# Moving the start addresses of the resident matmul operands by 8 to 240 bytes, stage by stage

## The chip, the cores and the metric

The kernel runs on one core of one Trainium2 chip. The metric is the device time of one execution in microseconds (us). Two executions of the kernel before took 2346.87 and 2346.46 us, a median of 2346.66 us.

Engines are named as in the profile: PE is TensorE's matmul side, PEld its weight loads, DVE is VectorE, ACT is ScalarE, POOL is GpSimd, SP is SyncE (it issues most DMAs here). SBUF is the on-chip memory of 128 partitions, PSUM the matmul's accumulators. In a matmul the *stationary* operand is loaded into the array first; the *moving* operand is then streamed from SBUF through it, a column at a time. "128x512" is a matmul whose moving operand has 128 partitions and 512 columns.

## The reference

One layer over 4096 prompt rows and 32 sample rows of width 1024, all float32. The large products are the input projection (`h @ w_in`, 1024 to 5120 columns; the pooling matrix is folded into one of its parts) and the output projection (`concat(a, b) @ w_out`, 2048 to 1024):

```python
def mixer_layer(x, pool_past, pos0, norm_g, w_in, ln_v_g, ln_v_b, w_spatial, b_spatial,
                w_pool, pool_scale, w_out):
    h = rmsnorm(x, norm_g)
    proj = jnp.einsum('btd,de->bte', h, w_in)
    u, v, z_a, xb, z_b = jnp.split(proj, [W_A, 2 * W_A, 3 * W_A, 3 * W_A + W_B], axis=-1)
    v_n = layernorm(v, ln_v_g, ln_v_b)
    a = u * chunk_mlp(v_n, w_spatial, b_spatial) * jax.nn.silu(z_a)
    x_ext = jnp.concatenate([pool_past.astype(xb.dtype), xb], axis=1)
    b = pool_mix(x_ext, pos0, w_pool, pool_scale) * jax.nn.silu(z_b)
    y = x + jnp.einsum('bte,ed->btd', jnp.concatenate([a, b], axis=-1), w_out)
    return y, x_ext[:, -POOL_STATE:], v_n
```

`chunk_mlp` multiplies 128 rows of v by a masked 128x128 matrix for each of 8 heads; `pool_mix` takes trailing means of 2, 4, 8 or 16 rows. The five outputs are the two final RMSNorms of y, two small state buffers and the sample's normalised v.

## The kernel before, in words

Every large product is done in a two-by-two block scheme with seven block products in place of eight (numbered q = 0 to 6, `NQ` = 7): operands are sums and differences of quarters, and `Combine` or `OutPair.multiply` adds the seven results up. Each operand is split into a high and a low part in the float32r format, and a block product is 12 matmuls: four pieces of 128 in the contracted dimension, and for each high x high, high x low and low x high.

One operand of every block product stays in SBUF for a whole stage: seven *slots*, one for each q (pool `slots`, helper `slot()` at L105). A slot is 16,896 bytes a partition, which is 33 x 512; the built program puts the first one at byte 18,432 of a partition, which is 36 x 512, so all seven begin at a multiple of 512 bytes. The slots are always the moving operand; what changes from step to step is the stationary one (`op` in the first stage, `wop` afterwards). The stages, in order of time:

- **v stage** (about 52 to 397 us): the slots hold the v columns of `w_in` (`wv`, L264). ACT and DVE write them (`weight_ops`), PE reads a row of 512 adjacent columns, 2048 bytes. In front of it lies the folding of the pooling matrix.
- **Blocks 0, 1, 2** (three stages of about 320 us from 397, 721 and 1040 us on): 1024 prompt rows each. A slot holds the row operands, loaded from `xops` by `Tokens.load` (L922, two DMAs of 1 MB a slot) or, for block 0, by `load_first` (L589, DMAs for two of the four row groups and a DVE and an ACT copy for the others). They are laid out as `(h j k t)`, and so a matmul's moving operand is four runs of 128 columns, each 512 bytes long and 2048 bytes from the next:

```python
return self.ops[q][:, :8 * HALF].rearrange("p (h j k t) -> p h k j t", h=2, j=4, t=P)[:, h, k]
```

- **Block 3, the last** (about 1359 to 1704 us): 1024 prompt rows and the 32 sample rows. A slot is filled to its end, as `(h k t)` with t = 528 columns (`WIDE`), and a row is taken in two matmuls of 264 columns, 1056 bytes each.
- **Output projection, z = 0 and z = 1** (about 1704 to 2026 and 2026 to 2338 us): the slots hold seven combinations of one half of `w_out`, loaded from `wops` by `load_out_weights` (L632, one DMA of 2 MB a slot). PE reads 512 adjacent columns; the very last step uses 256 at a time.

In each of blocks 0 to 2 the slots are read by 16 sets of weight columns, each set 7 x 12 = 84 matmuls, 1344 in all; the v stage (16 row pairs) and each half of the output projection (16 pairs) have the same count, block 3 twice as many of the narrow ones.

The order is written out in the program. Where two sets share the end or the beginning of a stage, `lagged` interleaves their steps as a0 a1 b0 a2 b1 a3 b2 a4 a5 b3 a6 b4 b5 b6. After step q of the last set of a stage the slot of q is free, and SP issues its load for the next stage at that point (L931, L634, L596); the new stage's first set reaches q = 6 ten steps after the old stage's last step. SP's queue also carries the weight loads (L956), which stand behind these. `prepare` has DVE and ACT make the stationary operands some steps ahead of PE.

Of the kernel before, what the change touches and what calls it, by code (L numbers as in the profile page):

```python
# [9 lines left out]
F32R = mybir.dt.float32r  # L10
# [5 lines left out]
P = 128  # L16
D = 1024
# [8 lines left out]
NB = 4  # L26
TB = SEQ // NB
HALF = TB // 2
EXT = DEC // 2
WIDE = HALF + EXT  # L30
TOT = SEQ + DEC
NQ = 7
WARM = 14


@with_exitstack
def stream_step(ctx: ExitStack, tc, x_prompt, x_sample, state_pool, norm_g, w_in, ln_v_g, ln_v_b,
# [18 lines left out]
    slots = ctx.enter_context(tc.tile_pool(name="slots", bufs=NQ))  # L56
# [45 lines left out]
        return y, guess + 3 * [lambda: stt(t, y, y, m, ALU.mult, ALU.mult),  # L102
                               lambda: stt(y, t, 1.5, y, ALU.add, ALU.mult)]

    def slot():  # L105
        return slots.tile([P, 2 * 4 * WIDE], F32R, tag="slot", name="slot")


    behind = []
# [101 lines left out]
    with ExitStack() as ph:  # L211
# [23 lines left out]
        def tr_tile():  # L235
            return ps_tr.tile([P, 512], F32, tag="tr", name="tr")

        g_bc = g_p.tile([P, D], F32, name="g_bc")
        first_ops = {}
# [9 lines left out]
        warm = tr_tile()  # L249
        for _ in range(WARM):  # L250
            tc.keep_in_program_order(nc.tensor.transpose(warm[:, :P], ident, ident))
# [9 lines left out]
                mm(dst, rows[ct], wraw[g // 2][:, 2 * (g % 2) + ct, :], start=ct == 0, stop=ct == 1)  # L261


        wv = [slot()[:, :8 * HALF].rearrange("p (h k n) -> p h k n", h=2, n=HALF) for _ in range(NQ)]  # L264

        v_raws = {}

# [86 lines left out]
        class Past:  # L354


            def load(self):
                self.st = half(), half()
                for z in range(2):
                    nc.gpsimd.memset(self.st[z][:HALO], 0.0)  # L360
                    nc.sync.dma_start(self.st[z][1:HALO], state_pool[0, 0, :, z * 512:(z + 1) * 512])
# [226 lines left out]

        def load_first(q):  # L589

            first_ops[q] = t = slot()
            dst = t[:, :8 * HALF].rearrange("p (h j x) -> p h j x", h=2, j=4)
            src = xops[0].rearrange("j p (q h x) -> q h p j x", q=NQ, h=2)
            n = 2 if q < NQ - 1 else 4
            for h in range(2):
                nc.sync.dma_start(dst[:, h, :n].bitcast(F32), src[q, h, :, :n])  # L596
            if n == 4:
                return
            nc.vector.tensor_copy(dst[:, :, pa.j], pa.ops[q])
            nc.scalar.copy(dst[:, :, pb.j], pb.ops[q])  # L600
# [4 lines left out]
        for n, (pair, q) in enumerate(lagged(pa, pb)):  # L605
            for step in {0: steps[:2], 1: steps[2:3], 2: steps[3:4], 4: steps[4:5], 6: steps[5:6], 7: steps[6:]}.get(n, []):
                step()
            if n == 1:
                norms([], [(v, P) for v in pairs[-3].v])
                pairs[-3].store()  # L610
            pair.product(q)
            if pair is pb:
                load_first(q)
# [16 lines left out]
    w_slots = {}  # L630

    def load_out_weights(z, q):  # L632
        w_slots[z, q] = t = slot()[:, :4 * D].rearrange("p (k h n) -> p k h n", k=4, h=2)
        nc.sync.dma_start(t.bitcast(F32), wops[z, q].rearrange("p k (h n) -> p k h n", h=2))  # L634

    class OutWeights:
# [227 lines left out]
    with ExitStack() as ph:  # L864
# [50 lines left out]
        class Tokens:  # L915
# [4 lines left out]
                self.groups = [(0, HALF)] if not self.last else [(0, WIDE // 2), (WIDE // 2, WIDE // 2)]  # L920

            def load(self, q):  # L922
                t = slot()
                self.ops[q] = t
                if self.last:
                    nc.sync.dma_start(t.bitcast(F32), xops_l[q].rearrange("p x t -> p (x t)"))
                    return
                src = xops[self.b].rearrange("j p (q h x) -> q h p j x", q=NQ, h=2)
                for h in range(2):
                    dst = t[:, h * 4 * HALF:(h + 1) * 4 * HALF].rearrange("p (j x) -> p j x", j=4)  # L930
                    nc.sync.dma_start(dst.bitcast(F32), src[q, h])  # L931
# [214 lines left out]
        for n in range(n_sets):  # L1146
# [9 lines left out]
            for s, q in order:  # L1156
                at += 1
                prepare(at + LEAD)
                while later:
                    (later.pop(0) or (lambda: None))()  # L1160
                for c, c0, w in cs[id(s)]:
                    s.product(c, q, c0, w)
                if n == 0 and q == 0:
                    behind.append(s)
                if s is g[-1] and groups[n + 1][0].stage != s.stage:
                    if n + 1 < n_sets:
                        groups[n + 1][0].tok.load(q)
                    else:
                        if q == 3:
                            groups[n_sets][1].begin([raw_tile(), raw_tile()], True)  # L1170
                        load_out_weights(0, q)
                if n == 0 and s is g[-1] and q in (3, 5):
                    next(constants, None)
                if s.kind == "gate" and q in (2, 4):
                    if q == 2:
                        s.t1 = []
                    s.t1.append(s.spatial(len(s.t1)))
                if s.kind == "gate" and q == 6 and s.tok.last:
                    s.spatial_sample()
                if q == NQ - 1:  # L1180
                    later.append(s.finish_gate() if s.kind == "gate" else s.finish_pool())
# [4 lines left out]
    with ExitStack() as ph:  # L1186
# [56 lines left out]
        for n in range(n_sets, len(groups)):  # L1243
# [6 lines left out]
            for m, (s, q) in enumerate(order):  # L1250
                at += 1
                prepare(at + LEAD)
                if m == 0 and n in samples:
                    samples[n].load()
                k = n - n_sets - 4
                if k == KT and m == 2:
                    sample_rows()
                if 0 <= k < KT and m in (0, 2):
                    state_load(k) if m == 0 else state_split()
                s.multiply(q)  # L1260
                if n == n_sets and s is g[0] and q == NQ - 1:
                    s.finish()
                if m == 2 and ended:
                    for x in ended:
                        x.finish()
                if s is g[-1] and n + 1 < len(groups) and groups[n + 1][0].stage != s.stage:
                    load_out_weights(1, q)
                if 0 <= k < KT and m == 6:
                    state_rows(k)
# [34 lines left out]
```

## Time and profile before

The profiled execution spans 2345.9 us, from its first to its last instruction; the other two executions took 2346.87 and 2346.46 us.

| | busy us | share of the span |
|---|---|---|
| PE, matmuls | 2328.8 | 99% |
| PEld, weight loads | 1981.3 | 84% |
| DVE | 1790.2 | 76% |
| ACT | 896.4 | 38% |
| POOL | 215.1 | 9% |
| DMA, 445.69 MB | | 190 GB/s on average |

A matmul's own duration in the profile runs from its start to the end of its drain and overlaps that of the next one, so the mean of one (389 ns for 512 columns) says how long one takes and not how fast they follow one another. How fast they follow is read from a stretch without gaps: the time from the first start to the last start, divided by their number less one. That quotient is called the *pitch* below. Times of windows are counted from the span's start.

### The profile page before, as it was taken

To read this page: it belongs to the slowest core of one execution; us is meant where nothing else is said; L and a number is where in the kernel's file an instruction comes from. 1 tells how busy PE (TensorE), PEld (TensorE's weight loads), DVE (VectorE), ACT (ScalarE), POOL (GpSimd) and SP (SyncE) were. 2 spreads that over 40 slices of the span, in tenths; PEclk is the share of its full clock that TensorE was granted. 3 is DMA by queue.
4 is the path that set the end of the run, shared out by engine and by line. 5 is a ranking of instruction groups with operands and counts; after the bars stand their busy time and mean duration, and the time that the engine had idled before them with its cause. 6 is when DMAs were issued, how large, how long until landed. Compare 5 with 4: busy or idle time off the path is not lost.

```text
span 2345.9 us, 32604 instructions
## 1 busy us (share of the span) xinstructions
PE 2328.8 (99%) x11936; PEld 1981.3 (84%) x11936; DVE 1790.2 (76%) x3318; ACT 896.4 (38%) x1603; POOL 215.1 (9%) x398
## 2 busy tenths in 40 slices
PE   8999999999999999999999999999999999999998
PEld 7878888888888888888888899999987878888877
DVE  7877786866787767877668876668777778688887
ACT  6545544433433333433334333334322333233333
POOL 1010000100021000111000110102200000000000
PEclk9999999999999999999999999999999999999999
DMA  8879977432448334483334472335587776955542
GB/s 309 316 241 279 275 255 245 142 104 89 149 144 296 99 100 134 135 300 122 108 108 148 177 262 87 101 100 164 223 294 265 252 257 232 360 171 169 159 137 90
DMA packets 325145, 445.69 MB, mean 190 GB/s; under 512 B 19324, under 2 KB 248444, under 8 KB 322296
## 3 DMA queue, kind: packets, MB, share of 16 engines
q1 hardware_dynamic: 273384, 355.05, 45.9%
q0 software_dynamic: 22288, 73.48, 8.3%
q10 hardware_dynamic: 29312, 15.08, 2.4%
q8 instruction: 94, 1.54, 0.3%
q14 instruction: 67, 0.55, 0.1%
HBM read 273.88 MB, written 169.66 MB: 189 GB/s over the span
## 4 chain that ended last, share of the span: by engine, by line
PE 95%; DMA 2%; DVE 2%; issue 0%; ACT 0%; SPq 0%; ACTq 0%; DVEq 0%
PE acc L193 66%; PE acc L712 8%; PE acc L713 8%; PE acc L714 8%; PE sp L998 2%; PE tr L473 1%; DMA wops<-raw 1%; DMA vt<-in_w_in_dram 1%; PE acc L261 0%; DMA op<-in_w_in_dram 0%; PE more L844 0%; PE more L843 0%; DVE wop L81 0%; DVE y L724 0%; PE acc L202 0%
## 5 line engine op out<-in xcount | busy, mean ns | idle before, releaser
L193 PE MATMUL acc<-slot,wop 128*128 128x512 f32 (+1 forms) x6720 | 1260.9, 348 | 1.0 <-DVE wop L81 1.0
L193 PEld LDWEIGHTS acc<-slot,wop 128*128 128x128 f32 x6720 | 1081.1, 188 | 156.5 <-DVE wop L81 1.4
L81 DVE TENSOR_TENSOR wop<-raw,wop 128x512 fp32r<-128x512 f32 (+1 forms) x510 | 353.4, 695 | 133.0 <-ACT wop L119 121.7
L119 ACT CAST wop<-raw 128x512 fp32r<-128x512 f32 x340 | 210.5, 622 | 384.4 <-PE acc L193 266.9
L712 PE MATMUL acc<-slot,wop 128*128 128x512 f32 x892 | 347.2, 389 | 1.5 <-DVE y L724 1.5
L713 PE MATMUL acc<-slot,wop 128*128 128x512 f32 x892 | 347.1, 389 | 0.0
L714 PE MATMUL acc<-slot,wop 128*128 128x512 f32 x892 | 347.0, 389 | 0.0
L193 PE MATMUL acc<-slot,op 128*128 128x512 f32 x1344 | 323.8, 395 | 0.3 <-ACT vt L167 0.2
L193 PEld LDWEIGHTS acc<-slot,op 128*128 128x128 f32 x1344 | 247.6, 188 | 51.9 <-ACT vt L167 0.7
L165 DVE TENSOR_TENSOR t<-acc,t 128x512 f32<-128x512 f32 (+1 forms) x320 | 186.7, 584 | 120.0 <-ACT t L174 65.5
L724 DVE TENSOR_TENSOR y<-acc,y 128x512 f32<-128x512 f32 x235 | 159.3, 687 | 72.6 <-PE acc L714 72.2
L712 PEld LDWEIGHTS acc<-slot,wop 128*128 128x128 f32 x892 | 167.4, 188 | 37.8 <-ACT wop L677 2.3
L714 PEld LDWEIGHTS acc<-slot,wop 128*128 128x128 f32 x892 | 167.4, 188 | 34.8
L713 PEld LDWEIGHTS acc<-slot,wop 128*128 128x128 f32 x892 | 167.4, 188 | 34.7
L677 ACT CAST wop<-raw 128x512 fp32r<-128x512 f32 x160 | 98.7, 622 | 175.2 <-PE acc L714 164.9
L81 DVE TENSOR_TENSOR wop<-sum,wop 128x512 fp32r<-128x512 f32 x200 | 136.9, 685 | 25.7 <-ACT wop L119 24.9
L1017 POOL DMA_DIRECT2D abT<-t x128 | 69.2, 541 | 843.2 <-DVE t L1029 622.7
L119 ACT CAST wop<-sum 128x512 fp32r<-128x512 f32 x136 | 84.5, 622 | 96.9 <-PE acc L193 72.0
L1040 DVE TENSOR_TENSOR t<-t 128x527 f32<-128x527 f32 (+3 forms) x160 | 111.1, 698 | 0.6
L677 ACT CAST wop<-sum 128x512 fp32r<-128x512 f32 x64 | 39.7, 622 | 119.5 <-PE acc L714 96.3
L174 ACT COPY t<-acc 128x512 f32<-128x512 f32 (+1 forms) x80 | 40.2, 504 | 107.1 <-PE acc L193 105.4
L115 DVE TENSOR_TENSOR sum<-raw 128x512 f32<-128x512 f32 x68 | 46.8, 688 | 44.7 <-DMA raw<-in_w_in_dram 44.1
(236 smaller groups left out, 1955.0 us busy)
## 6 DMA issues: line engine op xcount, KB each, us to landing
raw<-in_w_in_dram SPq DMA_DIRECT2D x102, 512.0 KB, 4.3
xops<-op SPq DMA_DIRECT2D x72, 512.0 KB, 6.1
abT<-t POOLq DMA_DIRECT2D x128, 256.0 KB, 3.8
raw<-abT SPq DMA_DIRECT2D x64, 512.0 KB, 5.0
slot<-xops SPq DMA_DIRECT2D x30, 1024.0 KB, 9.6
slot<-wops SPq DMA_DIRECT2D x14, 2048.0 KB, 9.7
xt<-in_x_prompt_dram SPq DMA_DIRECT2D x32, 512.0 KB, 5.0
raw<-v_all SPq DMA_DIRECT2D x32, 512.0 KB, 3.3
```

The costliest lines, as they stand in the source:

```text
L81: return nc.vector.tensor_tensor(out, src, hi.bitcast(F32), ALU.subtract)
L119: pair = nc.scalar.copy(hi, src), lo_part(lo, src, hi)
L165: add = lambda o, x, y: nc.vector.tensor_tensor(o, x, y, ALU.add)
L193: mm(acc, stationary(s, k), moving(m, k), start=fresh and n == 0, stop=n == len(terms) - 1, skip_group_check=True)
L677: nc.scalar.copy(t[:, 0], src)
L712: mm(acc, x[:, 0, k, :], w[:, k, 0, c], start=fresh and k == 0, stop=False, skip_group_check=True)
L713: mm(acc, x[:, 0, k, :], w[:, k, 1, c], start=False, stop=False, skip_group_check=True)
L714: mm(acc, x[:, 1, k, :], w[:, k, 0, c], start=False, stop=k == 3, skip_group_check=True)
L724: nc.vector.tensor_tensor(y, self.acc[bank], y, ALU.add)
L998: mm(sp[:, a, :], self.v[:, 4 * hf + a, :], WT[:, h, :], start=True, stop=True)
L1017: nc.gpsimd.dma_start(abT[row, :, t0:t0 + HALF], t[:, :HALF])
L1040: tt(nxt[:, lo:HALO + m], s[:, lo:HALO + m], s[:, lo - step:HALO + m - step], ALU.add)
```

## The change

`slot` takes a number of float32 columns that the tile's view begins late by, and each stage gives its own:

```diff
+SHIFT = (48, 56, 60, 0, 24, 40, 2)
...
-    def slot():
-        return slots.tile([P, 2 * 4 * WIDE], F32R, tag="slot", name="slot")
+    def slot(shift=0):
+        t = slots.tile([P, 2 * 4 * WIDE], F32R, tag="slot", name="slot")
+        return t[:, shift:] if shift else t
...
-        wv = [slot()[:, :8 * HALF].rearrange("p (h k n) -> p h k n", h=2, n=HALF) for _ in range(NQ)]
+        wv = [slot(SHIFT[6])[:, :8 * HALF].rearrange("p (h k n) -> p h k n", h=2, n=HALF) for _ in range(NQ)]
...
-            first_ops[q] = t = slot()
+            first_ops[q] = t = slot(SHIFT[0])
...
-        w_slots[z, q] = t = slot()[:, :4 * D].rearrange("p (k h n) -> p k h n", k=4, h=2)
+        w_slots[z, q] = t = slot(SHIFT[NB + z])[:, :4 * D].rearrange("p (k h n) -> p k h n", k=4, h=2)
...
-                t = slot()
+                t = slot(SHIFT[self.b])
```

| stage | shift in columns | start in bytes past a multiple of 512 | a matmul reads |
|---|---|---|---|
| v stage | 2 | 8 | 1 run of 2048 bytes |
| block 0 | 48 | 192 | 4 runs of 512 bytes |
| block 1 | 56 | 224 | 4 runs of 512 bytes |
| block 2 | 60 | 240 | 4 runs of 512 bytes |
| block 3 | 0 | 0 (its slots have no room) | 1 run of 1056 bytes |
| output, z = 0 | 24 | 96 | 1 run of 2048 bytes |
| output, z = 1 | 40 | 160 | 1 run of 2048 bytes |

Rows and runs in a slot are a multiple of 512 bytes apart in all of them but block 3, so every moving operand of a stage begins by the same distance past a multiple of 512. The tiles keep their addresses and sizes, the stationary operands and PSUM tiles too. No instruction is added, removed or moved on any engine or queue: the two built programs have the same instructions in the same order, and differ in the addresses at which DMAs, ACT and DVE write the slots and PE reads them.

## Prediction

> **What bounds the kernel now.** I read the page's table of engines first, then the waits of PE, then the chain of work that ended last, and last the stretches of each stage.
>
> ```profile
> PE 2328.8 (99%) x11936; PEld 1981.3 (84%) x11936; DVE 1790.2 (76%) x3318; ACT 896.4 (38%) x1603; POOL 215.1 (9%) x398
> PE acc L712 <- DVE y L724: 1.5, 2, 1.1
> PE 95%; DMA 2%; DVE 2%; issue 0%; ACT 0%; SPq 0%; ACTq 0%; DVEq 0%
> ```
>
> PE is busy for 2328.8 of 2345.9 us. The second row is one of the longest of PE's waits on another engine after the start-up: 1.5 us in two times. The chain (third row) is PE for 95% of the span. So nothing hides a change in the matmuls' own speed, and nothing else is worth much. What the change can touch is that speed, through where the moving operand begins, and the writing of the slots.
>
> The stages as windows (stretch in us, its length, PE busy and matmuls, granted clock, DMA share, GB/s), from the v stage to the end of the output projection:
>
> ```profile
> 51.80:396.90 345.10, 344.04 (x1631) 1.00 0.84 268
> 397.00:720.50 323.50, 322.55 (x1488) 1.00 0.45 147
> 720.60:1039.70 319.10, 319.10 (x1473) 1.00 0.46 154
> 1039.80:1358.90 319.10, 319.10 (x1473) 1.00 0.46 154
> 1359.00:1704.00 345.00, 345.00 (x2831) 1.00 0.44 152
> 1704.20:2025.70 321.50, 319.98 (x1410) 1.00 0.79 272
> 2025.70:2338.20 312.50, 312.44 (x1390) 1.00 0.48 161
> ```
>
> PE has no gap worth the name in any, and the clock is full in all of them. Blocks 0, 1 and 2 are within 4.4 us of one another. The pitch inside them comes from PE's timeline (start, time from first start to last end, line, operands, count):
>
> ```profile
> 701.83 16.48 PE L193 MATMUL acc<-slot,wop 128*128 128x512 f32 x72
> 1369.84 30.38 PE L193 MATMUL acc<-slot,wop 128*128 128x264 f32 x249
> 1749.81 0.39 PE L712 MATMUL acc<-slot,wop 128*128 128x512 f32 x1
> ...
> 1755.02 0.39 PE L714 MATMUL acc<-slot,wop 128*128 128x512 f32 x1
> 2335.11 0.28 PE L712 MATMUL more<-slot,wop 128*128 128x256 f32 x1
> ...
> 2337.86 0.28 PE L714 MATMUL more<-slot,wop 128*128 128x256 f32 x1
> ```
>
> - Block 0, four runs of 512 bytes, aligned: (16.48 - 0.39) / 71 = 226.6 ns.
> - Output projection, one run of 2048 bytes, aligned: 24 matmuls from the third row to the fourth, (1755.02 - 1749.81) / 23 = 226.5 ns. So breaking the operand into four runs costs nothing.
> - The last step, 256 columns, aligned: 24 matmuls, 2.75 / 23 = 119.6 ns. Two sizes give the price of a column: (226.6 - 119.6) / 256 = 0.418 ns, and 12.6 ns a matmul beside.
> - Block 3, 264 columns: (30.38 - 0.28) / 248 = 121.4 ns.
>
> The last one is the row on which my forecast rests, since **block 3 is already misaligned**. Its rows are 528 columns, 2112 bytes apart, which is 4 x 512 + 64, and its second matmul of a row starts 1056 bytes in, 2 x 512 + 32. Over h, k and the two halves its starts fall on all sixteen multiples of 32 past a multiple of 512, from 0 to 480. At the column price an aligned matmul of 264 would take 119.6 + 8 x 0.418 = 122.9 ns. It takes 121.4, which is 1.5 ns less. A start at a multiple of 32 bytes costs nothing there.
>
> **The change, part by part.** No instruction comes or goes, so every term is a number of matmuls times a change of pitch, all on the path.
>
> *Block 0 (192 bytes), block 1 (224), output z = 0 (96) and z = 1 (160).* All four shifts are multiples of 32, the class that block 3 shows at no cost. The matmuls are 4 x 1344 = 5376. Low end: the 1.5 ns that block 3 saves, 5376 x 1.5 = -8 us. High end from the same row is 0 for one run; for four runs I have no misaligned row, only that four aligned runs cost what one does. I take 0, the value that both rows give.
>
> *Block 2 (240 bytes).* 240 is 7 x 32 + 16, a class that the trace doesn't hold. Eight columns are 32 bytes, so if PE fetched 32 bytes at a time each of the four runs would need one fetch more, at most 4 x 8 x 0.418 = 13.4 ns a matmul, 1344 x 13.4 = 18.0 us. Low end as above, -2 us. I take 0: the nearest row, block 3's, shows no cost at any start, and 16 bytes is nearer to it than to anything else.
>
> *v stage (8 bytes).* One run, so one such fetch more would be 8 x 0.418 = 3.3 ns, 1344 x 3.3 = 4.5 us; low end -2 us. The nearest rows at an odd start are of another engine, DVE's window sums, which begin 1 to 15 columns past the tile's data, beside an aligned one:
>
> ```profile
> L1040 DVE TENSOR_TENSOR t<-t 128x527 f32<-128x527 f32 x64 | 44.9, 701 | 0.2
> L1040 DVE TENSOR_TENSOR t<-t 128x513 f32<-128x513 f32 x16 | 11.0, 689 | 0.0
> L1028 DVE TENSOR_TENSOR t<-t 128x512 f32<-128x512 f32 x48 | 32.9, 685 | 0.0
> ```
>
> 701 - 685 = 16 ns for 15 columns, about 1 ns a column whatever the start: reading off a line's start is free for DVE. I take 0 for PE too.
>
> [...]
>
> *Writing the slots.* In the v stage ACT and DVE write them at 8 bytes; before block 0 two copies of each slot's data do. DVE's rows above show odd starts at no cost, and the writing engines wait for PE elsewhere, not PE for them. I take 0.
>
> *The DMAs into the slots* start at 96 to 240 bytes. What hides them is the time between a slot's release and its next use. The tightest is block 1's last slot (SP's timeline: the issues of its two DMAs; and their median time to landing):
>
> ```profile
> 720.84 4.79 SPq L931 DMA_DIRECT2D slot<-xops  x2
> slot<-xops SPq DMA_DIRECT2D x2, 1024.0 KB, 15.4
> 691.00:739.00 48.00, 48.00 (x213) 1.00 1.02 375
> ```
>
> The slot is released at about 720.84, when the old block's last step ends, and read ten steps later: 10 x 12 x 0.2266 = 27.2 us, so at 748. It lands 15.4 us after an issue between 720.8 and 725.6, so by 736 to 741, 7 to 12 us early. The third row shows that DMA is full (share 1.02) in the 48 us in which the slots are reloaded, so a slower write lengthens these 48 us directly: the cover ends at 7 to 12 in 48, 15 to 25% slower. Below that the cost is 0, which I take.
>
> *Sum:* 0 us on the profiled execution's 2345.9. The runs' median is 0.8 us above that span, so the forecast is 2347 us. The ends of the bounds together: -12 and +22.5 us, 2335 and 2369.
>
> **The rivals.**
>
> *A fetch of 32 bytes (still within 2%).* Block 2 pays up to 18.0 and the v stage up to 4.5 us: 2352 to 2369. For it: nothing in the trace excludes it, as 1056 bytes from a multiple of 32 is always 33 whole fetches. Against it: none of block 3's starts, on 64 or off it, shows more than the column price.
>
> *A fetch of 64 bytes (slower).* Runs that begin 32 or 48 past a multiple of 64 would touch one unit more, 16 x 0.418 = 6.7 ns a run. Blocks 1 and 2: 4 runs x 6.7 x 2688 = 72 us; output: 6.7 x 2688 = 18; v stage: 6.7 x 1344 = 9; block 0, at 3 x 64, nothing. Together +99, 2446 us, slower. It decides as soon as a run's extra unit costs more than 47 / 99 of that, 3.2 ns. Against it: block 3's 1056 bytes would be paid as 17 units, 272 columns, 119.6 + 6.7 = 126.3 ns, and it takes 121.4. Only a mechanism bound to runs of 512 bytes that cross a boundary would escape that row.
>
> *A split fetch (slower).* If a start off 16 bytes made PE fetch every piece twice, the v stage would stream at half speed: 1344 x 512 x 0.418 = +288 us, 2635 us. It decides at a sixth of that. For it: no PE row here starts off 32 bytes. Against it: DVE's rows.
>
> *Late slots (slower).* At double the write time the 48 us become 96, and each of five stage changes waits some 48 - 10 = 38 us: +190. 2% (47 us) is reached at 19 us a change, where loads take 40% more. The v weights aren't loaded this way. [...]
>
> *Faster.* If a start off 512 really saves the 1.5 ns of block 3, the gain is 12 us, 2335, within 2%. To be faster by 2% it would have to be 47 us over 8064 - 1344 = 6720 matmuls, 7 ns of the 12.6 that a matmul has beside its columns. Nothing shows that. That the change does nothing is excluded: the addresses differ in the built program.
>
> **How the numbers follow.** Free starts (2335 to 2352): 0.62. A 32-byte fetch (2352 to 2369): 0.14. Late slots: 0.06, half of it under 2% above. A 64-byte unit or another cost per run: 0.09. A split fetch in the v stage or block 2: 0.07. Faster by over 2%: 0.02. Within 2% (about what a measurement of this kernel can tell from no change) are 0.62 + 0.14 + 0.03 = 0.79, slower 0.03 + 0.09 + 0.07 = 0.19, faster 0.02. The range goes from the low bound, 2335, past the 32-byte case to 2390, which holds most of the small cases of late slots: about 0.8 in all.
>
> **What would show it.** Read the changed kernel's windows by stage, each with its own shift. Right: every stage within 1 us of the rows above and a pitch of 226.6 ns in all of them. A 32-byte fetch: block 2 alone longer by up to 18 us. A 64-byte unit: blocks 1 and 2 longer by 36 us each and the output halves by 9, block 0 unchanged. A split fetch: the v stage alone, by up to 288. Late slots: waits of PE on a slot's DMA within 30 us of a stage's start, with the pitch unchanged behind. Block 3 keeps its addresses and must keep its 345.0 us. My forecast is wrong if a start on a multiple of 32 costs anything in the four-run stages, which block 3's single runs cannot show.

## The result and the profile after

The changed kernel takes 2402.02 us (2400.54 and 2403.5) against 2346.66: 1.0234 times as long, with a 95% interval of 1.0204 to 1.0263. Slower, where no change was forecast, and outside the range. The profiled execution spans 2401.7 us, 55.8 more than before.

The page after, the rows that answer to those of before: engines and the chain (line numbers in the rows below are two higher than before, since the helper grew by two).

```profile
PE 2385.0 (99%) x11936; PEld 1991.0 (83%) x11936; DVE 1797.3 (75%) x3318; ACT 897.4 (37%) x1603; POOL 202.1 (8%) x398
...
PE 95%; DMA 2%; DVE 1%; ACT 0%; issue 0%; SPq 0%; ACTq 0%; DVEq 0%
```

PE has the same number of matmuls, is as full as before and is still the chain. It has no new wait of more than 0.8 us. It is busy 56.2 us longer, so the matmuls themselves became slower. The windows by stage (stretch, its length, PE busy and matmuls, granted clock, DMA share, GB/s) show where; v stage, blocks 0 to 3, output z = 0 and 1:

```profile
53.60:404.20 350.60, 349.56 (x1631) 1.00 0.82 264
404.40:736.20 331.80, 330.94 (x1487) 1.00 0.44 144
736.40:1064.10 327.70, 327.70 (x1473) 1.00 0.45 150
1064.30:1395.90 331.60, 331.60 (x1473) 1.00 0.45 150
1396.10:1742.20 346.10, 345.32 (x2832) 1.00 0.44 149
1742.40:2071.40 329.00, 328.74 (x1410) 1.00 0.77 267
2071.60:2393.90 322.30, 322.30 (x1389) 1.00 0.46 155
```

Against the same rows before: +5.5, +8.3, +8.6, +12.5, +1.1, +7.5 and +9.8 us, 53.3 together. Another 1.8 us are in the start-up (the v stage begins at 53.6 in place of 51.8; the runs below began it between 50.5 and 52.5, so most of this is scatter). All six shifted stages pay, the unshifted block 3 hardly; the clock is full everywhere.

The pitch, read as in the prediction. First before, then after, the same stretch of block 2; then block 3 after:

```profile
1299.65 16.71 PE L193 MATMUL acc<-slot,wop 128*128 128x512 f32 x73
```

```profile
1299.79 16.50 PE L195 MATMUL acc<-slot,wop 128*128 128x512 f32 x69
1414.81 30.39 PE L195 MATMUL acc<-slot,wop 128*128 128x264 f32 x249
```

Before: (16.71 - 0.39) / 72 = 226.7 ns. After, at 240 bytes: (16.50 - 0.40) / 68 = 236.8 ns. Block 3 after: (30.39 - 0.28) / 248 = 121.4 ns, unchanged. Read for every stage from the single starts (the median at each of the twelve places of a block product, averaged), the pitch after is 233.2 ns at 8 bytes, 233.3 at 192, 224 and 96, 234.0 at 160 and 236.5 at 240. So, but for 240 bytes, nearly the same 6.7 ns come on top (5 in the v stage, which is at 228 with no shift), whether the shift is a multiple of 64, 32 or 8, and whether the operand is one run or four. 6.7 x 1344 = 9 us a stage is about what the windows show.

The slots' loads are not late. The DMAs into block 1's last slot, at 224 bytes, land as before:

```profile
slot<-xops SPq DMA_DIRECT2D x2, 1024.0 KB, 15.5
```

15.5 us from issue to landing, against 15.4. Over all 30 loads of 1 MB the median is 9.9 us against 9.6, and PE waits for none of them.

### The profile page after: what moved, and what is told of

The parts are those of the page before. It is cut to its first block, busy times and chain, and to the rows that moved or that the text cites. A ratio compares the mean times of both kernels' runs of the same rounds, so it can differ in the third digit from the quotient of the medians.

```text
span 2401.7 us, 32604 instructions
## 1 busy us (share of the span) xinstructions
PE 2385.0 (99%) x11936; PEld 1991.0 (83%) x11936; DVE 1797.3 (75%) x3318; ACT 897.4 (37%) x1603; POOL 202.1 (8%) x398
## 4 chain that ended last, share of the span: by engine, by line
PE 95%; DMA 2%; DVE 1%; ACT 0%; issue 0%; SPq 0%; ACTq 0%; DVEq 0%
PE acc L195 65%; PE acc L714 8%; PE acc L716 8%; PE acc L715 8%; PE sp L1000 2%; PE tr L475 1%; DMA wops<-raw 1%; DMA xt<-in_x_prompt_dram 1%; PE acc L263 0%; PE more L846 0%; DMA wops<-wop 0%; DMA vt<-in_w_in_dram 0%; PE more L845 0%; DMA part<-y 0%; DVE wop L82 0%
## 5 line engine op out<-in xcount | busy, mean ns | idle before, releaser
L195 PE MATMUL acc<-slot,wop 128*128 128x512 f32 (+1 forms) x6720 | 1291.0, 353 | 1.6 <-DVE wop L82 0.9
L714 PE MATMUL acc<-slot,wop 128*128 128x512 f32 x892 | 353.8, 397 | 0.3 <-DVE y L726 0.2
L716 PE MATMUL acc<-slot,wop 128*128 128x512 f32 x892 | 352.9, 396 | 0.0
L715 PE MATMUL acc<-slot,wop 128*128 128x512 f32 x892 | 352.4, 395 | 0.0
L195 PE MATMUL acc<-slot,op 128*128 128x512 f32 x1344 | 329.1, 400 | 0.3 <-ACT vt L169 0.2
L167 DVE TENSOR_TENSOR vt<-acc,vt 128x512 f32<-128x512 f32 x64 | 44.1, 688 | 47.8 <-ACT vt L176 32.2
```

The source lines that it names most:

```text
L167: add = lambda o, x, y: nc.vector.tensor_tensor(o, x, y, ALU.add)
L195: mm(acc, stationary(s, k), moving(m, k), start=fresh and n == 0, stop=n == len(terms) - 1, skip_group_check=True)
L714: mm(acc, x[:, 0, k, :], w[:, k, 0, c], start=fresh and k == 0, stop=False, skip_group_check=True)
L715: mm(acc, x[:, 0, k, :], w[:, k, 1, c], start=False, stop=False, skip_group_check=True)
L716: mm(acc, x[:, 1, k, :], w[:, k, 0, c], start=False, stop=k == 3, skip_group_check=True)
```

## The experiments

Two theories were left by the result (a third, C, late slots, is tested along with them). **A**: the moving operand's own start decides, by some multiple X of bytes. **B**: what decides is the *distance* between the moving operand's start and that of the stationary operands, which all lie at multiples of 512 here. Each stage has its own shift, so that one kernel tests up to six values. Unless said otherwise a kernel is the changed one with another `SHIFT` (blocks 0 to 3, output z = 0 and 1, v stage; in columns of 4 bytes), and pitches of stages are read as the last ones above. The first four ran on one chip beside the kernel before, at 2348.64 us. All but the two with ratios are single runs; the kernel before was between 2346.0 and 2349.7 us throughout.

**Which starts pay, 1.**

```diff
-SHIFT = (48, 56, 60, 0, 24, 40, 2)
+SHIFT = (32, 64, 16, 0, 32, 16, 1)
```

> Shifts in bytes: block 0 128, block 1 256, block 2 64, output z=0 128, z=1 64, v stage 4. The changed kernel's pitch (first start to first start of matmuls that follow one another) is 233.3 ns against 226.7 in five of its six shifted stages, 6.7 ns x 1344 = 9 us a stage. Theory A (the moving operand's start alone): it is paid by every start that is no multiple of X. X = 512: all six stages at 233.3, about 2401 us. X = 256: block 1 back at 226.7, 2392 us. X = 128: blocks 0 and 1 and output z=0 at 226.7, 2374 us. X = 64 is excluded by the 192 bytes of the changed kernel. Theory B (distance between the moving operand's start and the stationary one's, which lie at multiples of 512): the same stages as A here, it is told apart elsewhere. Theory C (late slots): pitch 226.7 with waits behind each stage's start.

Measured: 2381.52 us. Block 1 at 256 bytes is back at 226.8 ns. The others: 231.7 at 128 (both stages), 229.0 at 64 (both), 237.8 at 4. So X is 256, and the waits of theory C aren't there; but the price is no constant: 64 costs 2.3 ns, 4 bytes 11, which is why the time is under the 2392 us of X = 256.

**Which starts pay, 2.**

```diff
+SHIFT = (4, 8, 128, 0, 64, 128, 64)
```

> Shifts in bytes: block 0 16, block 1 32, block 2 512, output z=0 256, z=1 512, v stage 256. Theory A with X = 512: blocks 0 and 1, output z=0 and the v stage at 233.3 ns, block 2 and output z=1 at 226.7: 4 x 9 = 36 us more than before, 2383 us. X = 256: blocks 0 and 1 alone, 2365 us. X = 128: the same 2365 us. Theory B: as A here. If the price came from using another part of the slot at all and not from alignment, block 2 and output z=1 would pay too: 2401 us.

Measured: 2360.72 us. 512 bytes (block 2, at 226.7 ns, and z = 1) and 256 bytes (z = 0, v stage) pay nothing, in one run or in four; 16 bytes 231.8 ns, 32 bytes 233.3. Using another part of the slot costs nothing. X = 256 again.

**The stationary operand moved.** The decisive one.

```diff
+SHIFT = (0, 24, 64, 0, 0, 24, 0)
...
+    pad_p = pool("pad_p", 1)
+    pad_p.tile([P, 24], F32, tag="pad", name="pad")
     op_p = pool("wop_p", 7)
```

> A pad of 96 bytes ahead of the stationary tiles of blocks 0 to 3 and of the output projection (wop), so that these begin 96 past a multiple of 512; the v stage's stationary tiles stay. Moving operands: block 0 at 0, block 1 at 96, block 2 at 256, output z=0 at 0, z=1 at 96, v stage at 0. Theory A (start of the moving operand alone): block 0, output z=0 and v stage at 226.7 ns, block 1 and output z=1 at 233.3, block 2 by the X found: 2365 or 2374 us. Theory B (distance of the two starts): block 0, output z=0 and block 2 at 233.3 since the distance is 96 there (or 160), block 1 and output z=1 back at 226.7 although both operands are off 512: about 2374 us. If either operand off 512 costs by itself, all five stages are at 233.3: 2392 us.

Measured: 2375.27 us, as B said. Block 2's stretch, moving at 256 and stationary at 96:

```profile
1299.73 16.56 PE L195 MATMUL acc<-slot,wop 128*128 128x512 f32 x70
```

(16.56 - 0.39) / 69 = 234.3 ns for a moving operand that cost nothing at 256 in the two runs before. Block 0 and z = 0, with the moving operand untouched at 0, are at 234.1 and 234.3. Block 1 and z = 1, with both operands at 96, are at 226.8 and 227.0. A stretch of block 1:

```profile
999.75 16.48 PE L195 MATMUL acc<-slot,wop 128*128 128x512 f32 x72
```

(16.48 - 0.39) / 71 = 226.6 ns. Theory A falls: an aligned moving operand pays and a misaligned one doesn't. The sign fits too. The three dear stages have a distance of 160 modulo 256 (0 - 96, or 256 - 96), and their 234.1 to 234.3 ns are those of the changed kernel's z = 1 at 160 (234.0), not those at 96 (233.3).

**Why 240 is dearer.**

```diff
+SHIFT = (60, 28, 62, 0, 60, 52, 60)
```

> Shifts in bytes: block 0 240, block 1 112, block 2 248, output z=0 240, z=1 208, v stage 240. In the changed kernel 240 in block 2 cost 236.5 ns, 9.8 above the aligned pitch, where the five others cost 6.7. Run theory: the rest comes from four runs with a start off 32 bytes, so block 0 at 240 is at 236.5 again, blocks 1 (112) and 2 (248) too, and the one-run stages, v and output z=0 at 240 and z=1 at 208, at 233.3: about 2347 + 3 x 13.2 + 3 x 9 = 2414 us. Place theory: the rest comes from a start in the last 16 bytes below a multiple of 256, so v and output z=0 at 240 show 236.5 too, block 1 at 112 and output z=1 at 208 show 233.3: 2347 + 4 x 13.2 + 2 x 9 = 2418 us.

Measured: 2406.45 us. 240 bytes cost 236.5 ns in four runs (block 0) and in one (z = 0, v stage) alike, so the run theory falls; 208 is at 235.0 and 248 the dearest of all, here in block 2:

```profile
1299.67 16.72 PE L195 MATMUL acc<-slot,wop 128*128 128x512 f32 x69
```

(16.72 - 0.39) / 68 = 240.1 ns. And block 1 at 112 bytes shows 226.7, which neither theory had.

**The width of the matmul, and four more distances.**

```diff
+SHIFT = (12, 20, 44, 0, 0, 60, 36)
...
-            self.product(q, self.acc[own], slice(0, 512), own == q)
+            mid = 264 if self.z == 0 else 256
+            for c in (slice(0, mid), slice(mid, 512)):
+                self.product(q, self.acc[own][:, c], c, own == q and c.start == 0)
```

> Two questions in one kernel. (1) Why block 3's row of 264 columns showed no price: in the output projection z=0 (moving operand at 0) each matmul of 512 columns is made as one of 264 and one of 248 columns, in z=1 (moving operand at 240, the dearest start but 248) as two of 256. Theory 'columns': a moving operand off the stationary one's distance streams slower only where the matmul is wide enough to outlast the weight load beside it (188 ns), so at 256 columns and 240 bytes the pitch is at most the 119.6 ns of the aligned 256 columns, and 264 columns aligned take 121 to 123 ns, like block 3's. Theory 'fixed price': 240 bytes cost 9.8 ns at 256 columns too, 129.4 ns, and 264 aligned columns take 114 to 116 ns, block 3 having paid 6.7 all along. (2) Is there a distance below 226.7 ns: block 0 at 48, block 1 at 80, block 2 at 176, v stage at 144 bytes; theory B (distance modulo 256 decides) has no order for them and says only that each has a constant pitch of its own between 226.7 and 240; a pitch under 226.7 would give a faster kernel. The split itself adds 1344 matmuls a half at about 12.6 ns, 17 us each: about 2347 + 34 + 4 stages at 0 to 18 us, 2381 to 2440 us.

Measured: 2462.58 us. The pitch at 256 columns and 240 bytes (z = 1), from two rows of PE's timeline with 24 starts from the first to the last:

```profile
2199.82 0.28 PE L715 MATMUL acc<-slot,wop 128*128 128x256 f32 x1
...
2202.51 0.28 PE L714 MATMUL acc<-slot,wop 128*128 128x256 f32 x1
```

2.69 / 23 = 117.0 ns, 2.6 *less* than the 119.6 of 256 aligned columns. And 264 aligned columns (z = 0), twelve of them from 1801.15 to the next part's start at 1802.60:

```profile
1801.15 0.28 PE L714 MATMUL acc<-slot,wop 128*128 128x264 f32 x1
...
1802.60 0.28 PE L714 MATMUL acc<-slot,wop 128*128 128x248 f32 x1
```

1.45 / 12 = 120.8 ns, about block 3's 121.4. The "columns" theory holds: at these widths the distance costs nothing, or gains, and at 512 it costs 2 to 13 ns. The last step of the changed kernel, 256 columns at 160 bytes, agrees (24 starts):

```profile
2390.98 0.28 PE L714 MATMUL more<-slot,wop 128*128 128x256 f32 x1
...
2393.69 0.28 PE L716 MATMUL more<-slot,wop 128*128 128x256 f32 x1
```

2.71 / 23 = 117.8 ns, 1.8 less than aligned. At 256 columns distance 0 is thus the slowest of these three, and at 512 the fastest. This answers why the row of block 3 misled. Of the new distances 48, 144 and 176 are at 233.2 to 233.3 ns and 80 at 231.3; none is below 226.7. The time is above the expected 2440 us, because PE ran dry in the split z = 0 (it waits 31.1 us in all on DVE's additions into `y`):

```profile
1735.00:2128.00 393.00, 348.27 (x2709) 0.93 0.65 222
```

PE is busy for 348 of 393 us and its clock fell to 0.93 on average. That is the cost of the split, and says nothing on distances.

**Both operands off by the same 96 bytes.** The pad of the third experiment, and all shifts of blocks and output at 24 columns.

```diff
+SHIFT = (24, 24, 24, 0, 24, 24, 0)
```

> The slots of blocks 0, 1, 2 and of both output halves begin at 96 bytes, and the pad of 96 bytes ahead of the stationary tiles (wop) is there too, so both operands are off a multiple of 512 and of 256 by the same 96; v stage as before the change. Theory B (distance modulo 256): pitch 226.7 ns in all five stages, 2347 us, no change against before. Theory A (moving operand alone): five stages at 233.3, 2347 + 45 = 2392 us.

Measured: 2347.89 us against 2348.15 for the kernel before, a ratio of 1.0 with an interval of 0.999 to 1.0009. Block 2's stretch is the one of before to the last digit:

```profile
1299.62 16.71 PE L195 MATMUL acc<-slot,wop 128*128 128x512 f32 x73
```

Five of the six stages have their moving operands off a multiple of 256, and the price is gone. Theory B, timed.

**All at 112.**

```diff
+SHIFT = (28, 28, 28, 0, 28, 28, 28)
```

> All six shifted stages begin at 112 bytes, the one distance off a multiple of 256 that showed the aligned pitch (226.7 ns in block 1 of an earlier run). Theory B with a pattern of its own for each distance: 226.7 ns in every stage, at most 1 ns more on average, 2347 to 2358 us. If 112 was a chance of that one stage: 233 ns in the others, about 2390 us.

Measured: 2370.3 us, a ratio of 1.009 (1.0073 to 1.0107). Neither expectation: in the blocks and the output the pitch goes 231, 237, 225 in turn, 231.0 on average:

```profile
1299.73 16.57 PE L195 MATMUL acc<-slot,wop 128*128 128x512 f32 x71
```

(16.57 - 0.39) / 70 = 231.1 ns. The v stage, also at 112, stays at the 227 ns (median) of the kernel before. So 112 has two patterns; which one a stage takes the distance alone does not settle.

**Only the low halves of the stationary tiles at 96.** High and low halves get pools of their own, with the pad between; all slots at 0.

```diff
+SHIFT = (0, 0, 0, 0, 0, 0, 0)
...
+    pad_p = pool("pad_p", 1)
+    pad_p.tile([P, 24], F32, tag="pad", name="pad")
+    low_p = pool("low_p", 7)
...
-        return op_p.tile([P, 2, 4, P], F32R, tag="wop", name="wop")
+        return op_p.tile([P, 4, P], F32R, tag="wop", name="wop"), low_p.tile([P, 4, P], F32R, tag="wop", name="wop")
```

> All slots at 0. The high halves of the stationary tiles lie at multiples of 256, the low halves in tiles of their own 96 bytes past one, so that of the three matmuls of a piece (high x high, high x low, low x high) only the third has a stationary operand at a distance. Theory 'load beside' (the moving stream meets the load of the next stationary operand, which the profile shows starting 3 ns after each matmul's start): the pitch of the second of the three, during which the low half is loaded, rises to 233 to 238 ns, the first and third stay at 226.7; mean 229 ns, about 2347 + 2 to 4 ns x 6720 = 2360 to 2375 us. Theory 'own pair' (a matmul meets its own stationary operand): the third rises, the first and second stay. Stores of the output weights go in two DMAs of 256 KB here and some small tiles move to another pool, off PE's path.

Measured: 2393.73 us, more than either form foresaw. All three matmuls of a piece rise: high x high 233.1 ns, high x low (during which the low half is loaded) 231.7, low x high 232.7, as averages over blocks and output. One stationary operand in three at another distance spoils the pitch of all. So it can't be said from this which load a matmul meets, only that the price isn't private to the pair that is off.

**Shorter weight loads.**

```diff
+SHIFT = (60, 28, 28, 0, 0, 40, 0)
...
             for k in range(4):
-                mm(acc, x[:, 0, k, :], w[:, k, 0, c], start=fresh and k == 0, stop=False, skip_group_check=True)
-                mm(acc, x[:, 0, k, :], w[:, k, 1, c], start=False, stop=False, skip_group_check=True)
-                mm(acc, x[:, 1, k, :], w[:, k, 0, c], start=False, stop=k == 3, skip_group_check=True)
+                full = P if k == 0 else m
+                mm(acc[:full], x[:, 0, k, :full], w[:, k, 0, c], start=fresh and k == 0, stop=False, skip_group_check=True)
+                mm(acc[:m], x[:, 0, k, :m], w[:, k, 1, c], start=False, stop=False, skip_group_check=True)
+                mm(acc[:m], x[:, 1, k, :m], w[:, k, 0, c], start=False, stop=k == 3, skip_group_check=True)
```

with `m = P // 2`. Half of the output rows is left out here, so a matmul's load and what it writes are both halved, in eleven of twelve.

> In the output projection eleven of each twelve matmuls use 64 of the 128 stationary columns (half of the output rows is left uncomputed there), so the weight load beside each is shorter (134 ns where a load of 64 columns stands in the profile of before, 188 for 128); the moving operand keeps its 512 columns. z=0 at 0 bytes, z=1 at 160. With full loads the pitches are 226.7 and 234.0 ns. Theory 'collision with the load': the price of 160 bytes falls with the load, to about half, 3 to 4 ns (z=1 less z=0). Theory 'moving stream alone, timed by its distance': the price stays 7.3 ns. The pitch of z=0 itself is open: 226.7 if the 13 ns beside the columns are a fixed cost, about 220 if they grow with the stationary columns. Blocks 0, 1, 2 at 240, 112, 112 bytes repeat block 1 at 112 behind a block at 240, which held 226.7 ns in one run, where another run gave 225, 231 and 237 in turn (231 on average): if the state left by the stage ahead decides, block 1 is at 226.7 again. Time: output faster by 0 to 18 us, blocks as before, about 2347 + 13 + 0 to 12 + 5 to 10.

Measured: 2366.28 us. With eleven of twelve loads halved the pitch is 229.7 ns on average at distance 0 and 227.3 at 160, and the price of 160 bytes, 7.3 ns with full loads, is gone; it is even 2.4 ns the other way. From one full load to the next in z = 1, twelve matmuls, and then over two such rounds in z = 0:

```profile
2209.93 0.39 PE L716 MATMUL acc<-slot,wop 128*128 128x512 f32 x1
...
2212.65 0.40 PE L716 MATMUL acc<-slot,wop 128*128 128x512 f32 x1
```

```profile
1850.25 0.40 PE L716 MATMUL acc<-slot,wop 128*128 128x512 f32 x1
...
1855.76 0.40 PE L716 MATMUL acc<-slot,wop 128*128 128x512 f32 x1
```

2.72 / 12 = 226.7 ns and 5.51 / 24 = 229.6 ns. The theory in which the moving stream pays by itself falls. The collision theory had the direction and not the size (3 to 4 ns were expected to stay), and distance 0 is no longer the better of the two, as its even pitch of 226.7 is broken up (224 to 236 ns from matmul to matmul). The 13 ns beside the columns didn't shrink with the load. Blocks 1 and 2 at 112 bytes are at 226.7 ns again, behind a block at 240.

## Why the prediction was wrong

*What bounds the kernel.* Right: PE's pitch is the time, and every stage is all PE. The result is six stages' pitches and nothing else.

*Blocks 0 and 1 and the output halves, taken at 0.* This is the step that failed. The row of block 3 was read rightly in the main: at 264 columns starts at all multiples of 32 bytes cost under 1 ns on average. It was carried to 512 columns, and there it doesn't hold. The fifth experiment shows both sides: 264 aligned columns take 120.8 ns, about block 3's 121.4, and 256 columns at 240 bytes take 117.0 and not more than the aligned 119.6, while the same 240 bytes cost 9.8 ns at 512. The trace of before had no misaligned matmul of 512 columns with a full load beside it. The bound "high end 0" had no row of that width under it; to say so and to widen the range was what the row allowed. The low end had none either: the 1.5 ns that block 3 seemed to save came from the column price, which puts 264 aligned columns at 122.9 ns where they measure 120.8. The prediction had named a cost at a multiple of 32 in the four-run stages as the sign of its being wrong. The sign came, but the one-run output halves pay as well: what block 3 lacked was the width, and not the four runs.

*Block 2, at most 13.4 ns for four runs.* It pays 9.8, inside the bound, and for another reason: runs don't count. The fourth experiment has the same 236.5 ns for one run and for four.

*v stage, at most 3.3 ns.* Its pitch rises from 228 to 233 ns and its window by 5.5 us, a little over the 4.5 of the bound. The rows of DVE say nothing on PE. Nor is the price one of starts off 16 bytes: 192, 224, 96 and 160 bytes, all multiples of 16, pay 6.6 to 7.3 ns.

*The DMAs into the slots, hidden.* Right: 15.5 us to landing against 15.4, and PE waits for none. That row is under 1% slower, and the median of all loads of 1 MB (9.9 us against 9.6) 3%, where the cover had room for 15 to 25%.

*The rivals.* The 64-byte unit had the side of the result and, by chance, a size of 6.7 ns. Its mechanism is refuted: block 0 at 192 bytes pays too, and blocks 1 and 2 don't pay four times. The 32-byte fetch falls because stages at multiples of 32 pay. The split fetch and the late slots didn't occur, and no stage got faster. None of the rivals had the stationary operand in it. That was the blind spot: the change was described, and thought of, as a matter of one operand's address, while the profile of before shows a weight load beside every matmul. This is a moment of block 1 before (start, time, engine, line):

```profile
799.80 1.29 PE L193 MATMUL acc<-slot,wop 128*128 128x512 f32 x5
...
800.03 0.87 PEld L193 LDWEIGHTS acc<-slot,wop 128*128 128x128 f32 x4
```

One load starts per matmul, about 3 ns behind it by the single starts, and lasts 188 of its 227 ns. So the two run side by side in step; that the addresses then fix the distance between what they read is argued from this and not seen in the trace.

*What is shown and what isn't.* Shown: at 512 columns and with full loads the price depends on the distance between the two starts modulo 256 bytes (experiments 1, 2, 3 and 6: 226.7 to 227.0 ns at 0, 256 and 512 and with both operands at 96, 234.1 to 234.3 in the three stages that the pad of experiment 3 put 160 apart). At 256 columns neither of the distances read, 160 and 240, pays it (117.8 ns in the last step of the changed kernel and 117.0 in experiment 5, against 119.6 at 0). With halved loads (a load of 64 columns takes 134 ns in the trace of before, one of 128 takes 188) 160 doesn't pay it either, at 227.3 ns, but distance 0 then takes 3 ns more, 229.7; only these two were tried, and the load alone isn't isolated there, since the same edit halves what a matmul writes. That the two reads collide was the author's estimate of the cause; no run shows it. Open: why the price is 2 ns at 64 bytes and 13 at 248, why 112 has two patterns, why the order turns round at 256 columns, and why, with one stationary operand in three off, all three matmuls of a piece rise (231.7 to 233.1 ns). The kernel before, at distance 0, has the lowest steady pitch of the nineteen tried, with 112 bytes in one of its two patterns beside it; no faster version came out of the runs.

## What to carry to other kernels

Where two operands are streamed side by side by instructions that start in step, try the distance between their addresses, and not only the alignment of either: for matmuls of 512 columns here, equal remainders modulo 256 bytes kept 226.6 to 227.0 ns, with both at 0 and with both at 96. A row that shows no price is proof only for its own shape; before carrying it to another width, name the work that runs beside it in both shapes and see whether it is covered in the same way.

## What the runs showed of the hardware

Pitch of a 128x512 float32r matmul with a full weight load beside it, by the distance in bytes between the moving and the stationary operand's start:

| distance | ns | distance | ns | distance | ns |
|---|---|---|---|---|---|
| 0, 256, 512 | 226.7 | 80 | 231.3 | 176, 192, 224 | 233.3 |
| 4 | 237.8 | 96 | 233.3 | 208 | 235.0 |
| 8, 144 | 233.2 | 112 | 226.7 or 231.0 | 240 | 236.5 |
| 16 | 231.8 | 128 | 231.7 | 248 | 240.0 |
| 32, 48 | 233.3 | 160 | 234.0 to 234.3 | 64 | 229.0 |

The values at 4, 8 and 144 are from the v stage, which has transposes between its matmuls and is at 228 ns with distance 0. The commonest price, 6.7 ns, is as much as 16 columns at 0.418 ns; no run shows whether that is more than chance.

No run here has these matmuls without a load beside them, so what a load costs at distance 0 is not shown. At most other distances the pitch is 2 to 13 ns of 227 longer. This goes by the stationary operand's place as well (block 0, its moving operand at 0, rose from 226.7 to 234.1 ns when the stationary one moved by 96 bytes), so the matmul and the load are not independent there.
